# First 1024 tokens' keys, queries and half of the output gates by seven products of block sums, head norm folded into w_out, left operands split one by one, 43 working tiles

## The chip, the cores and the metric

The kernel runs on one core of a Trainium2 chip. The metric is the device time of one launch in microseconds (us). Three runs of the kernel before took 2398.47, 2396.38 and 2397.98 us; their median is 2397.98 us. The profile is of one more execution.

## The reference

One encoder layer on 2048 tokens of width 1024, in float32. The part that matters here is the mLSTM mixer at its start:

```python
xn = rmsnorm(h, norm_mix)
u = xn @ w_in                                  # 2048 x 1024 times 1024 x 3088
q, k, v, o, g = split(u, [512, 1024, 2048, 3072])
k = k * 128 ** -0.5                            # 4 heads of 128
h_fwd = mlstm_scan(q, k, v, g[0], g[1])        # 16 chunks of 128 tokens
h_bwd = flip(mlstm_scan(flip(q), flip(k), flip(v), flip(g[2]), flip(g[3])))
h = h_fwd + h_bwd
h = h * rsqrt(mean(h ** 2 per head) + EPS) * head_norm
h = h * sigmoid(o)
mix = h @ w_out
```

After it come a residual add, a square-ReLU MLP (1024 to 4096 to 1024), a gated embedding term and a last norm.

## The kernel before, in words

**Products.** Every float32 product is made of three TensorE products. An operand is split into a rounded high part (`hi`, cast by ScalarE, the profile's ACT) and a rest (`lo`, subtracted by VectorE, DVE), and `mm3` issues hi·hi, hi·lo and lo·hi into one PSUM bank. A 128x512 output over 1024 inputs thus takes 8 x 3 = 24 matmuls.

**Two ways to multiply.** A *slab job* (`slab_job`, `feat_group`) takes 128 columns of `w_in` and gives them for 1024 tokens in two groups of 24 matmuls, named `psf`. A *pair job* (`pair_job`, `products`) takes 256 columns for 1024 tokens as a 2 by 2 block product with seven block products in place of eight (`SEVEN`): sums S1 to S4 of the left blocks (the weights) and T1 to T4 of the right blocks (the tokens), each product 12 matmuls, named `pa`, `pb`, `pc`. One pair job is 84 matmuls; the two slab jobs with the same output are 96. `Left.preps` makes the sums (tiles `sa`) and splits them (tiles `op`) in six steps: S1 and S2 are split as one 128x1024 operand, and S3 and S4 as another. `run7` runs pair jobs one after another and weaves the next job's six steps between the current job's seven products.

**Order of the first stage.** The second 1024 tokens come first: values (`psv`), then keys, queries and all output gates in eight pair jobs (`pairs1`, with T1 to T4 made by `TokensA`). Then the first 1024 tokens: values; then slab jobs, four for the keys (k), six for the output gates (o0 to o5), the first halves of the four query slabs (`qa`); and last `fin`, a list written out by hand (`TR`) that holds the slabs o6 and o7 and the other query halves (`b0` to `b3`) beside the loads and splits of `w_out` (`a0`.., `c0`..) and the first forward chunk. The token tiles of the first half are prepared during `pairs1` by `Early`: norm, transposition in blocks through DRAM (`mix_d`), and `tr`, which multiplies by the norm gain and splits.

**The backward scan.** From the last group of values on, 15 backward state updates are laid between the slabs (`bwd_steps`: load `kt` and `vst`; split v into `vh`, `vl` and scale keys into `wk`; 12 matmuls `pu`, new state `Cn`, split into `Chi`, `Clo`, stored to `cb_d`). Each update is three steps, and the list `slots` says before which slab group a step stands. Stores of the first half's keys, queries and gates and of `cb_d` go through GpSimd's queue (POOL), loads through SyncE's queue (SP). Both are served in order.

**Later stages.** 14 forward chunks with the output projection (`pso`), then 32 pair jobs for the MLP's first matrix (`up_job`, whose sums are made on POOL at L468 to L474 and whose class `Left1` is a `LeftW`), then the second matrix (`down_job`, `Left2`), then the last stage.

**Gates and head norm.** `o_evac` and `o_pair` take the sigmoid on ACT and multiply by `head_norm` on DVE (`g_hn`). The rows of `w_out` are split without a factor.

**Buffers.** Working tiles of 4 KiB a partition come from one pool `H` of 39 (`NH`), load tiles from a pool `O` of 7. A scheduler puts the instructions of each engine in a fixed order when the program is built, by priority and by tiles that are free; on the chip every engine runs its list in that order and waits at each instruction for what it needs. All calls through the recording class have line L98 or L100 in the profile.

Of the kernel before, what the change touches and what calls it, by code (L numbers as in the profile page):

```python
# [16 lines left out]
P = 128  # L17
# [4 lines left out]
H = 4  # L22
# [7 lines left out]
NH = 39  # L30
# [5 lines left out]
def hybrid_mlstm_kernel(  # L36
# [216 lines left out]
    class Prep:  # L253
# [50 lines left out]
        def norm1(self, j):  # L304
# [4 lines left out]
            for g, sl in rowc["mix"]:  # L309
                V.scalar_tensor_tensor(xs[:, sl], self.raw[j][:, sl], r[:, 0:1], g, op0=ALU.mult, op1=ALU.mult)  # L310
# [53 lines left out]
    class Early(Prep):  # L364
# [3 lines left out]
        def __init__(self, load, gain, name):  # L368
            super().__init__(load, gain)
            self.d = dram.tile([32, 32, 4, P], F32, name=name)  # L370
            self.z = [None] * 4

        def norm(self):
# [5 lines left out]
            for j in range(4):  # L379
                V.tensor_scalar_mul(self.raw[j], self.raw[j], r[:, j:j + 1])  # L380
# [9 lines left out]
        def tr(self, k):  # L390
            t = Ht("xT", [P, 2, 512], F32R)
            g = self.gain[:, k:k + 1]
            z = self.z[k // 2][:, k % 2]
            A.activation(t[:, 0], z, AF.Copy, scale=g)
            V.scalar_tensor_tensor(t[:, 1], z, g, t[:, 0].bitcast(F32), op0=ALU.mult, op1=ALU.subtract)
# [53 lines left out]
    class Left:  # L449

# [4 lines left out]
        def preps(self, eng, eng2=None):  # L455
# [29 lines left out]
            by_row = lambda x, i, k: x[:, i, k]  # L485
            return [s12, op(["A11"], lambda: self.r[0][:, :, :P], by_col),
# [8 lines left out]

# [27 lines left out]

    class Job7:
# [4 lines left out]

    def run7(jobs, deep=None):  # L530

        def dma(i):
            if i < len(jobs):
                jobs[i].left.dma()
        for i, j in enumerate(jobs):
            if i == 0:
                dma(1)
            if deep is None or i + 2 <= deep:
                dma(i + 2)
            if deep is not None and i + 2 >= deep:  # L540
                dma(i + 3)
            nxt = jobs[i + 1].prep if i + 1 < len(jobs) else []

            def both(g, post):
                def f():
                    g()
                    for h in post:
                        h()
                return f
            weave([both(g, p_) for g, p_ in zip(j.groups, j.post)], nxt + j.side)  # L550
# [15 lines left out]
    kty = {}  # L566

    def store(c, dst, src):
        (SP if c >= 8 else G).dma_start(dst, src)

    def k_shuffle(t, h, c0):

        for m in range(2):
            if h == 0:
                kty[c0, m] = Ht("y", [P, 8, H, 32])
            y = kty[c0, m]
            V.transpose(y[:, :, h, :], t[:, 2 * m:2 * m + 2].rearrange("p c (b i) -> p (c b) i", i=32))
            if h == H - 1:
                for a in range(4):
                    (G if c0 >= 8 else SP).dma_start(kt_d[(c0 + 2 * m) * P:(c0 + 2 * m + 2) * P, a].rearrange("(b i) e -> i b e", i=32),  # L580
                                y[32 * a:32 * a + 32].rearrange("i b h j -> i b (h j)"))
                del kty[c0, m]

    def kq_evac(qk, h):
        def f(ps, c0):
            t = St("ev", [P, 4, P])
            tv = as_(ps, t)
            if qk == 0:
                A.activation(tv, ps, AF.Copy, scale=DK ** -0.5)
            else:  # L590
                V.tensor_copy(tv, ps)
            store(c0, kq_d[c0:c0 + 4, :, qk, h, :].rearrange("c p t -> p c t"), t)
            if qk == 0:
                k_shuffle(t, h, c0)
        return f

    def o_evac(j):
        def f(ps, c0):
            t = St("ev", [P, 4, P])
            act(as_(ps, t), ps, AF.Sigmoid)  # L600
            V.tensor_scalar_mul(t, t, gains["hn"][:, j:j + 1])
# [181 lines left out]
    def v_load(c):  # L783
        t = Ht("vst", [P, D])
# [27 lines left out]
    def bwd_steps(c):  # L812
        s = {}

        def load():
            s["kt"] = kt_load(c, Ot)
            s["v"] = v_load(c)
# [14 lines left out]
    ta_d = dram.tile([4, 2, P, 2, 512], F32, name="ta_d")  # L832

# [56 lines left out]
    def pair_job(B_, blk, col, finish, scale=None):  # L890

        e = {}

        def after(i, ps):
            t = St("ev", [P, 512])
            if i in (0, 2, 3, 6):
                if scale is None:
# [867 lines left out]
```

## Time and profile before

| | us |
|---|---|
| median of three runs | 2397.98 |
| the profiled execution, its own time | 2398.35 |
| its span on the core | 2396.6 |
| PE (TensorE matmul) busy | 2364.5 |
| DVE (VectorE) busy | 1565.9 |
| ACT (ScalarE) busy | 1165.9 |
| POOL (GpSimd) busy | 629.9 |

Times of the trace are counted from the span's start. 1.75 us of the execution's own time lie outside of the span. PEld is the weight load, which overlaps PE. A group's "mean ns of one" is the length of one instruction; matmuls overlap their neighbours, so that the distance from one start to the next is the cost of one, and not its length.

### The profile page before, as it was taken

The page shows a single profiled execution, that of the slowest core. Times are in us where ns is not written, and L with a number is a line of the kernel's source. Part 1 is how long each engine was busy: PE and PEld are TensorE (multiplying, and loading weights), DVE is VectorE, ACT ScalarE, POOL GpSimd, SP SyncE. Part 2 cuts the span into 40 slices and gives each one's busy share as a digit, 9 for nine tenths or more (in the row PEclk, how much of TensorE's full clock was granted, in tenths as well). Part 3 has the DMA queues.
Part 4 walks back from the last instruction along what each step waited for, and adds up shares of the span by engine and source line. Part 5 has one row for each costly group of instructions (what it writes and reads, how often), then busy time and mean ns, then how long its engine had stood idle before and what let it go on. Part 6 is the DMA issues. An engine that isn't in the chain of part 4 may idle for free.

```text
span 2396.6 us, 31587 instructions
## 1 busy us (share of the span) xinstructions
PE 2364.5 (99%) x11225; PEld 1951.6 (81%) x11225; DVE 1565.9 (65%) x2612; ACT 1165.9 (49%) x2168; POOL 629.9 (26%) x679
## 2 busy tenths in 40 slices
PE   8999999999999999999999999999999999999998
PEld 6988988788889887888888888787888888888886
DVE  6677545557778887567685544767666667666665
ACT  5234434437788874343353333444444444455554
POOL 0041121124333324446533332111111111111121
PEclk9999999999999999999999999999999999999999
DMA  5676656868768883456673332568686776796453
GB/s 168 229 230 191 192 149 222 281 222 291 232 226 294 276 269 110 132 174 206 213 228 106 106 113 73 174 135 195 143 188 165 170 170 154 173 217 176 136 138 87
DMA packets 273896, 440.66 MB, mean 184 GB/s; under 512 B 48921, under 2 KB 182425, under 8 KB 273738
## 3 DMA queue, kind: packets, MB, share of 16 engines
q1 hardware_dynamic: 211466, 308.48, 39.5%
q0 software_dynamic: 61984, 129.64, 23.3%
q8 instruction: 88, 1.44, 0.3%
q14 instruction: 70, 0.57, 0.1%
q10 hardware_dynamic: 288, 0.52, 0.1%
HBM read 262.87 MB, written 175.50 MB: 183 GB/s over the span
## 4 chain that ended last, share of the span: by engine, by line
PE 59%; DVE 1%; issue 1%; DMA 0%; ACT 0%; POOL 0%; ACTq 0%; DVEq 0%; POOLq 0%
PE pa L100 29%; PE pb L100 14%; PE pg L100 7%; PE pc L100 7%; PE pl L100 2%; DVE op L100 0%; DMA wst<-in_mlp_w 0%; DVE raw L100 0%; DVE z L100 0%; DVE e L100 0%; ACT op L100 0%; PE pt L100 0%; ACT e L100 0%; DVE h L100 0%; POOL sa L474 0%
## 5 line engine op out<-in xcount | busy, mean ns | idle before, releaser
L100 PE MATMUL pa<-op 128*128 128x512 f32 x3360 | 823.6, 394 | 3.9 <-ACT e L100 2.3
L100 PEld LDWEIGHTS pa<-op 128*128 128x128 f32 x3360 | 629.4, 188 | 155.9 <-ACT e L100 4.8
L100 PE MATMUL pb<-op 128*128 128x512 f32 x1632 | 407.5, 394 | 0.8 <-DVE op L100 0.8
L100 PEld LDWEIGHTS pb<-op 128*128 128x128 f32 x1632 | 306.1, 188 | 73.3 <-DVE op L100 1.1
L100 DVE TENSOR_TENSOR op<-sa,op 128x1024 fp32r<-128x1024 f32 (+2 forms) x176 | 188.9, 1079 | 142.3 <-ACT op L100 109.2
L100 ACT CAST op<-sa 128x1024 fp32r<-128x1024 f32 (+2 forms) x176 | 156.6, 895 | 188.0 <-PE pb L100 95.2
L1303 POOL DMA_DIRECT2D h_d<-o x96 | 94.9, 1033 | 529.5 <-DVE o L100 443.4
L100 ACT COPY e<-pa 128x512 f32<-128x512 f32 x160 | 93.8, 587 | 277.6 <-PE pa L100 277.0
L100 PE MATMUL pc<-op 128*128 128x512 f32 x768 | 191.8, 394 | 0.2 <-DVE op L100 0.2
L100 PEld LDWEIGHTS pc<-op 128*128 128x128 f32 x768 | 144.1, 188 | 34.4 <-DVE op L100 0.6
L100 PE MATMUL psf<-xT,whi 128*128 128x512 f32 x512 | 161.5, 396 | 0.0
L100 PE MATMUL psv<-whi,xT 128*128 128x272 f32 (+2 forms) x720 | 160.9, 317 | 0.0
L100 ACT CAST op<-wst 128x512 fp32r<-128x512 f32 x112 | 92.5, 834 | 114.4 <-DVE op L100 59.9
L100 DVE TENSOR_TENSOR op<-wst,op 128x512 fp32r<-128x512 f32 x112 | 123.7, 1107 | 31.4 <-ACT op L100 18.0
L468 POOL TENSOR_TENSOR sa<-wst 128x512 f32<-128x512 f32 x32 | 58.8, 1837 | 263.9 <-PE pb L100 167.3
L100 PEld LDWEIGHTS psv<-whi,xT 128*128 128x128 f32 x720 | 118.3, 188 | 9.2 <-ACT xT L100 0.3
L100 PE MATMUL psv<-wlo,xT 128*128 128x272 f32 (+2 forms) x360 | 113.8, 316 | 0.0
L100 PEld LDWEIGHTS psf<-xT,whi 128*128 128x128 f32 x512 | 95.8, 189 | 21.5
L100 DVE TENSOR_TENSOR op<-hst,op 128x384 fp32r<-128x384 f32 (+1 forms) x96 | 65.4, 687 | 64.6 <-ACT op L100 45.1
L100 PE MATMUL pso<-whi,hThi 128*128 128x512 f32 x256 | 102.2, 400 | 2.9 <-ACT nt L100 1.4
L100 PE MATMUL psf<-xT,wlo 128*128 128x512 f32 x256 | 101.4, 396 | 0.0
L100 PE MATMUL pg<-whi,xTh 128*128 128x512 f32 x256 | 101.3, 397 | 0.0
(267 smaller groups left out, 4378.6 us busy)
## 6 DMA issues: line engine op xcount, KB each, us to landing
wst<-in_mlp_w SPq DMA_DIRECT2D x96, 512.0 KB, 4.9
h_d<-o POOLq DMA_DIRECT2D x96, 512.0 KB, 14.0
hid_d<-e SPq DMA_DIRECT2D x128, 256.0 KB, 2.4
hst<-hid_d SPq DMA_DIRECT2D x64, 384.0 KB, 7.0
wst<-in_mlstm_w_in SPq DMA_DIRECT2D x44, 512.0 KB, 5.6
vst<-v_d SPq DMA_DIRECT2D x31, 512.0 KB, 4.6
raw<-in_x SPq DMA_DIRECT2D x16, 512.0 KB, 6.7
kq<-kq_d SPq DMA_DIRECT2D x16, 512.0 KB, 3.6
```

Source lines behind the costliest of these rows:

```text
L100: r = f(*a, **kw)
L468: eng.tensor_tensor(s[:, 0], r1[:, :, P:], r2[:, :, P:], op=add_)
L1303: G.dma_start(rows(h1_d, 2 * q + i), o[i], accum_op=add_)
```

## The change

1. The first 1024 tokens' keys, queries and output gates o0 to o3 become six pair jobs (`pairs0`). Their T1 to T4 are made on POOL from the tiles in `mix_d` while `pairs1` runs and are kept in DRAM (`tm_d`); the plain right blocks are the token tiles themselves (`Mixed`). Their left sums are made on POOL (`left.preps(G)`). `Early` now multiplies by the norm gain in its norm, so `tr` is a plain split.
2. `fin` holds the slabs o4 to o7, both halves, in place of o6, o7 and the query halves. Four token tiles (first half of the inputs of tokens 512 to 1023), which no pair job reads, are dropped and loaded again for them.
3. The backward updates are side steps of the six pair jobs, four steps in each and three in the second.
4. For every left operand made from weights (`pairs1`, `pairs0` and the 32 `up` jobs) S1 to S4 are split one by one (`single`): three steps stand in the job before, three in the job itself.
5. `head_norm` goes into the split of `w_out`; the gates' DVE multiply is gone.
6. `NH` is 43, and the GpSimd DMA scratch is 4096 bytes a partition. A chunk's load of `cb_d` is issued behind its mask (`dma_c`); the backward `vst` uses pool `O`.

```diff
-NH = 39
+NH = 43
...
     class Left:
-
+        single = False
...
+            if n > 2 and self.single:
+                sums = {"S1": lambda: self.s[0][:, 0], "S2": lambda: self.s[0][:, 1],
+                        "S3": lambda: self.s[1][:, 0], "S4": lambda: self.s[1][:, 1]}
+                sop = {nm: op([nm], f, one) for nm, f in sums.items()}
+                return [[s12, op(["A11"], lambda: self.r[0][:, :, :P], one)],
+                        [op(["A12", "A22"], lambda: self.r[1], by_col)],
+                        [s34, sop["S2"]], [sop["S1"]], [sop["S3"]], [sop["S4"]]]
...
+    class Mixed(Summed):
+        def get(self, nm, k):
+            if nm[0] == "B":
+                pr, k = self.e[int(nm[2]) - 1], k + 4 * (int(nm[1]) - 1)
+                return pr.hi[k], pr.lo[k]
+            return super().get(nm, k)
...
+    LEAD = 3
...
+            if j.left.single:
+                for at, fs in enumerate(j.prep[LEAD:]):
+                    main[at][:0] = fs
+            nxt = []
+            if nx and nx.left.single:
+                for at, fs in enumerate(nx.prep[:LEAD]):
+                    main[7 - LEAD + at][:0] = fs
+            elif nx:
+                nxt = nx.prep
...
     def o_evac(j):
...
             act(as_(ps, t), ps, AF.Sigmoid)
-            V.tensor_scalar_mul(t, t, gains["hn"][:, j:j + 1])
...
-        return Job7(left, B_, 4, after)
+        return Job7(left, B_, 4, after, None if blk else left.preps(G))
...
+    def wo_prep(k):
+        wo[k].prep(None, gains["hn"][:, k:k + 1])
...
-        jobs[b, "k"] = [slab_job(pa[b], b, KC + h * P, kq_evac(0, h)) for h in range(H)]
-        jobs[b, "q"] = [slab_job(pa[b], b, QC + h * P, kq_evac(1, h), (ps_mm, (ps_tr, ps_mm)[b])) for h in range(H)]
-        jobs[b, "o"] = [slab_job(pa[b], b, OC + j * P, o_evac(j)) for j in range(KD)]
+    jobs[0, "o"] = o = [slab_job(pa[0], 0, OC + j * P, o_evac(j)) for j in range(4, KD)]
...
+    def pairs_of(B_, b, n):
+        return [kq_pair(B_, b, qk, hp) for qk in range(2) for hp in range(2)] + [o_pair(B_, b, jp) for jp in range(n)]
+    pairs1, pairs0 = pairs_of(xa, 1, 4), pairs_of(xm, 0, 2)
...
+    for job, n in zip(pairs0, (4, 3, 4, 4, 4, 4)):
+        job.side += steps[at:at + n]
+        at += n
...
-    run(seq)
+    run([jobs[0, "v"][1], jobs[0, "v"][0]])
+    run7(pairs0)
+    run([fin])
...
-    nc = _bacc.Bacc("TRN2", target_bir_lowering=False, num_devices=1)
+    nc = _bacc.Bacc("TRN2", target_bir_lowering=False, num_devices=1, dynamic_dma_scratch_size=4096)
```

Over the whole program TensorE's list has 11,159 matmuls before and 11,087 after: 576 `psf` fewer, 504 `pa`, `pb` and `pc` more.

The first place is GpSimd's list where the keys of the first 1024 tokens begin. Before (`v_d`, `kq_d` and `cb_d` are stores of values, of keys and queries, and of backward states):

```order
L569 DMA v_d<-ev 4x32x512 x2
L828 DMA cb_d<-Chi 128x1032
L828 DMA cb_d<-Clo 128x1032
L569 DMA kq_d<-ev 128x4x128 x2
L828 DMA cb_d<-Chi 128x1032
```

and after:

```order
L864 DMA cb_d<-Chi 128x1032
L864 DMA cb_d<-Clo 128x1032
L466 TENSOR_TENSOR sa<-wst 128x512
L632 DMA kq_d<-ev 128x4x128
L467 TENSOR_TENSOR sa<-sa,wst 128x512
L632 DMA kq_d<-ev 128x4x128 x2
L471 TENSOR_TENSOR sa<-wst 128x512
L472 TENSOR_TENSOR sa<-wst,sa 128x512
```

A queue that held only stores now also holds the four block sums of the next pair job, between stores that wait for evacuated tiles.

The second place is DVE's list in the same stretch. Before (`ev` are evacuated tiles, `y` the transposed keys, `wlo` the rests of the next slab's weights):

```order
L100 COPY ev<-psv 128x512
L100 SCALAR_TENSOR_TENSOR Cn<-Cn,dcb,pu 128x258 x4
L100 TENSOR_TENSOR Clo<-Cn,Chi 128x1032
L100 TENSOR_TENSOR wlo<-wst,whi 128x1024
L100 STREAM_TRANSPOSE y<-ev 128x8x32 x2
L100 MEMSET vh 128x4x2
```

and after, in the first pair job:

```order
L100 TENSOR_TENSOR ev<-pc,ev 128x512
L100 STREAM_TRANSPOSE y<-ev 128x8x32 x2
L100 TENSOR_TENSOR op<-z,op 128x1024 x2
L100 TENSOR_TENSOR op<-sa,op 128x512
L100 TENSOR_TENSOR op<-z,op 128x1024 x2
L100 SCALAR_TENSOR_TENSOR Cn<-Cn,dcb,pu 128x258 x4
L100 TENSOR_TENSOR ev<-pa,ev 128x512
L100 TENSOR_TENSOR ev<-pb,ev 128x512
L100 TENSOR_TENSOR Clo<-Cn,Chi 128x1032
```

Between two backward updates DVE now has splits of T3 and T4 (`op<-z`), splits of left sums (`op<-sa`) and adds of products (`ev`), where it had one weight split and two transposes.

The third place is ACT's list in `fin`. Before (`mb` are the first chunks' decay masks, an exponential; `ev<-psf` here is a gate's sigmoid):

```order
L100 ACTIVATE ev<-psf 128x512
L100 ACT_TABLE_LOAD
L100 ACTIVATE mb<-mb,gcol 128x128 x9
L100 CAST pTh<-mb 128x512
L100 ACTIVATE mb<-mb,gcol 128x128 x2
```

and after:

```order
L100 ACTIVATE ev<-psf 128x512 x3
L100 ACT_TABLE_LOAD
L100 ACTIVATE mb<-mb,gcol 128x128 x8
L100 ACT_TABLE_LOAD
L100 ACTIVATE ev<-psf 128x512
L100 ACT_TABLE_LOAD
L100 ACTIVATE wk<-kt,wcol 128x128 x4
L100 CAST pTh<-mb 128x512 x2
```

Sigmoids and exponentials now alternate in `fin`, and ACT's list has 43 table loads in all where it had 37.

251 lines of the change are left out of this document (119 added, 132 removed).

## The prediction

> **What bounds the kernel now.** I read the page first, then busy time by stage, then waits and timeline where a stage is not full.
>
> ```profile
> span 2396.6 us, 31587 instructions
> PE 2364.5 (99%) x11225; PEld 1951.6 (81%) x11225; DVE 1565.9 (65%) x2612; ACT 1165.9 (49%) x2168; POOL 629.9 (26%) x679
> ```
>
> PE is busy for all but 32.1 us of its span. A gain must come from fewer matmuls, or from shorter ones; the other engines matter only where they become late. By stage (columns: busy us and count of PE, PEld, DVE, ACT, POOL; granted clock; share of the DMA engines; GB/s):
>
> ```profile
> 113.90:270.00 156.10, 156.10 (x676) 126.18 (x675) 105.28 (x175) 73.84 (x111) 37.73 (x64) 1.00 0.70 215
> 367.40:521.70 154.30, 151.76 (x710) 125.31 (x709) 88.73 (x193) 63.33 (x103) 32.19 (x50) 0.99 0.74 243
> 521.70:620.00 98.30, 93.42 (x500) 78.75 (x499) 66.04 (x117) 63.88 (x158) 40.34 (x48) 1.00 0.78 270
> 907.00:1440.00 533.00, 530.29 (x2284) 427.90 (x2283) 332.76 (x350) 205.57 (x288) 232.55 (x160) 1.00 0.49 155
> ```
>
> These are the pair jobs of the second half; the slab jobs that the change replaces, from the first `psf` to the last one ahead of o6 (I call it the middle stage); `fin` with the first chunks; and the first MLP matrix. The pair jobs leave PE no idle time with DVE at 67%. The middle stage has 2.54 us idle, `fin` and after it 4.88, the `up` jobs 2.71.
>
> What one matmul costs is seen in the timeline, from start to start. Two rows of slab work and two of pair work:
>
> ```profile
> 400.37 0.63 PE L100 MATMUL psf<-xT,whi 128*128 128x512 f32 x2
> ...
> 419.18 0.63 PE L100 MATMUL psf<-xT,whi 128*128 128x512 f32 x2
> ```
>
> ```profile
> 1001.88 5.70 PE L100 MATMUL pa<-op 128*128 128x512 f32 x24
> 1007.42 2.94 PE L100 MATMUL pc<-op 128*128 128x512 f32 x12
> ```
>
> Between the first two lie 27 rounds of three matmuls: 18.81 / 81 = 0.232 us each. The 24 of the pair job take 5.54 us, 0.231 each. Both ways pay the same for a matmul.
>
> **The matmuls removed.** Twelve slabs (4 k, 4 q, o0 to o3) of 48 matmuls are 576; six pair jobs of 84 are 504. 72 x 0.232 = 16.7 us leave PE, and PE is the path there, so this is the gain unless others are late. The built order has exactly 72 fewer, so a rival by which the saving isn't made has no chance.
>
> **What a wait costs.** The middle stage had one, for the operands of a backward update:
>
> ```profile
> PE pu L100 <- ACT wk L100: 2.0, 1, 2.0
> PE pu L100 <- DVE vl L100: 0.6, 1, 0.6
> ```
>
> ```profile
> 436.69 0.39 PE L100 MATMUL pu<-vh,wk 128*128 128x258 f32 x1 [1.97 <-ACT wk L100]
> 437.65 0.39 PE L100 MATMUL pu<-vl,wk 128*128 128x258 f32 x1 [0.57 <-DVE vl L100]
> ...
> 439.60 1.05 PE L100 MATMUL psf<-xT,whi 128*128 128x512 f32 x2
> ...
> 440.88 1.05 PE L100 MATMUL psf<-xT,whi 128*128 128x512 f32 x2
> ...
> 442.14 0.63 PE L100 MATMUL psf<-xT,whi 128*128 128x512 f32 x2
> ```
>
> PE waited 1.97 + 0.57 = 2.54 us. Behind that, two rounds took 1.28 and 1.26 us in place of 0.70, so another 1.1 us went to a halved clock. One late update is thus 3.7 us. The cause stands in two windows:
>
> ```profile
> 425.00:435.00 10.00, 9.72 (x42) 7.51 (x40) 1.72 (x2) 1.06 (x3) 2.47 (x4) 1.00 1.01 377
> 435.00:445.00 10.00, 7.74 (x31) 6.37 (x32) 8.04 (x20) 6.63 (x13) 1.86 (x3) 0.83 0.80 282
> ```
>
> The DMA engines were full for 10 us, DVE and ACT idle and waiting for data, and then all came at once. [...]
>
> This wait goes with the slabs: -3.7. What is late next are the updates in their new place.
>
> **DVE in the middle stage.** Of its 88.7 us these go:
>
> ```profile
> L100 DVE TENSOR_TENSOR wlo<-wst,whi 128x1024 fp32r<-128x1024 f32 x15 | 18.0, 1218 | 0.4 <-ACT whi L100 0.4
> L100 DVE TENSOR_SCALAR ev<-ev,g_hn 128x512 f32<-128x512 f32 x12 | 5.8, 484 | 12.4 <-ACT ev L100 12.3
> L100 DVE COPY ev<-psf 128x512 f32<-128x512 f32 x3 | 2.1, 689 | 7.2 <-PE psf L100 7.2
> ```
>
> Four of the weight splits (4.9) stay for o4 to o7, so 21.0 us go. What comes is priced by the pair jobs of the second half:
>
> ```profile
> L100 DVE TENSOR_TENSOR op<-wst,op 128x512 fp32r<-128x512 f32 x6 | 4.1, 689 | 3.3 <-ACT op L100 3.3
> L100 DVE TENSOR_TENSOR op<-wst,op 128x1024 fp32r<-128x1024 f32 x6 | 7.3, 1224 | 2.7 <-ACT op L100 2.4 <-PE pb L100 0.3
> L100 DVE TENSOR_TENSOR ev<-pa,ev 128x512 f32<-128x512 f32 x6 | 4.1, 692 | 3.9 <-PE pa L100 3.9
> L100 DVE TENSOR_TENSOR op<-z,op 128x1024 fp32r<-128x1024 f32 x4 | 4.8, 1210 | 0.8 <-ACT op L100 0.8
> ```
>
> A job splits A11 and S1 to S4 (5 x 0.689), A12 with A22 (1.224), and adds three products (3 x 0.692): 6.75 us, six jobs 40.5. T3 and T4 add 4.8, the four token tiles split again 2.8. DVE then has 88.7 - 21.0 + 48.1 = 115.8 us to do while PE has 154.3 - 2.5 - 1.1 - 16.7 = 134.0. That alone is 86%.
>
> The left sums on POOL are new beside it. The `up` jobs show what that does:
>
> ```profile
> L100 DVE TENSOR_TENSOR op<-wst,op 128x1024 fp32r<-128x1024 f32 x26 | 37.2, 1432 | 10.5 <-DMA wst<-in_mlp_w 5.2 <-PE pb L100 3.9 <-PE pa L100 0.9
> L100 DVE TENSOR_TENSOR op<-wst,op 128x512 fp32r<-128x512 f32 x26 | 27.7, 1067 | 9.6 <-ACT op L100 8.5
> L468 POOL TENSOR_TENSOR sa<-wst 128x512 f32<-128x512 f32 x26 | 46.9, 1802 | 183.8 <-PE pb L100 133.1 <-PE pa L100 29.9 <-DVE op L100 13.8
> L474 POOL TENSOR_TENSOR sa<-wst,sa 128x512 f32<-128x512 f32 x26 | 40.1, 1543 | 0.0
> ```
>
> The same two splits take 0.378 and 0.208 us more there. Five short ones and a long one are 2.1 us a job, 12.6 for six: 128.4 of 134.0 us, 96%. The two key jobs have T3 and T4 (4.8) and all the transposes:
>
> ```profile
> L100 DVE STREAM_TRANSPOSE y<-ev 128x256 f32<-128x256 f32 x16 | 6.2, 422 | 11.0 <-ACT ev L100 11.0
> ```
>
> Without these 11.0 us a job has 117.4 / 6 = 19.6 us of DVE for 134.0 / 6 = 22.3 of PE, 88%; a key job on average 25.1, 113%.
>
> DMA is no better off. The stage moved 243 GB/s x 154.3 us = 37.5 MB at share 0.74. The same stores, states and loads, plus 2 MB for T3 and T4, in 134 us are 295 GB/s, a share of 0.90 if it grows alike; the keys' transposed stores also become twice as many of half the size. The 10 full us above came at 377.
>
> So some updates will be late. Below: none, 0. Above: each of the 11 in the stage, 11 x 3.7 = 41. I take two, one in each key job, since DVE is over 100% in those alone: +7.4. PE's list is fixed, so behind a late update the whole next product waits; DVE's `Cn` and the store to `cb_d` wait with it.
>
> **`fin`.** The matmuls are the same in number. ACT gets six more table loads, and four more evacuations that DVE had:
>
> ```profile
> L100 ACT ACT_TABLE_LOAD x1 | 1.3, 1283 | 0.0
> ```
>
> 6 x 1.283 = 7.7 us. ACT was busy 65% of the 98.3 us, so most lie beside PE's work. Where PE already waited for the first chunk's chain, they don't:
>
> ```profile
> PE pn L100 <- DVE xt L100: 1.4, 1, 1.4
> PE pso L100 <- ACT nt L100: 1.4, 1, 1.4
> ```
>
> Below, DVE's waits vanish with its multiplies: -1.4. Above, all loads: +7.7. I take two loads, those ahead of the second chunk's exponentials: +2.6.
>
> **The rest, each at nothing.** Splitting S1 to S4 one by one costs DVE 4 x 0.689 - 2 x 1.224 = 0.3 us a job, covered in the `up` jobs by 200 us of idle DVE; from -2.7 (their idle time) to +3.7 (one late operand). The sums on POOL and the gain in `Early`'s norm fall in the second half's pair jobs, where DVE has 51 us to spare; 0 to +3.7. Head norm in the split of `w_out` changes a subtraction into a subtraction with a factor. The load of `cb_d` behind the mask has most of a chunk, some 20 us, to land. [...]
>
> **Sum.** -16.7 - 3.7 + 7.4 + 2.6 = -10.4. The profiled execution took 2398.35, the median is 0.37 lower: 2397.98 - 10.4 = 2387.6.
>
> **Rivals.**
>
> *No update is late and ACT's loads are hidden.* For it: in the chunks after 620 us DVE and ACT were both busy 80% and PE lost under 2 of 287 us (below). Against: 96% isn't 80%. 2397.98 - 20.4 = 2377.6. Chance 0.18.
>
> ```profile
> 620.00:907.00 287.00, 285.06 (x1721) 251.48 (x1720) 228.29 (x458) 229.41 (x613) 96.93 (x122) 1.00 0.77 256
> ```
>
> *The gain is spent.* About five late updates, 18.5, plus 2.6 against 20.4: 2398.7. For it: the DMA share of 0.90. Against: an update's loads are issued a whole update ahead, and 11 us of matmuls lie between most updates. Chance 0.20.
>
> *DVE becomes the bound of the middle stage, and the kernel is slower.* Let a sum on POOL keep DVE out for its whole time. The two rows of L468 and L474 give (1.802 + 1.543) / 2 = 1.67 us, 24 sums 40.1, so DVE needs 155.9 us for 134.0 of PE. The 21.9 us between are waits of 2.54 us, 8.6 of them, and each brings its 1.1 of slow clock, 9.5 more: 2397.98 - 20.4 + 21.9 + 9.5 + 2.6 = 2411.6. It decides from the fifth late update on, where 18.5 + 2.6 pass 20.4; from the seventh the loss passes 0.2%. Against: in the `up` jobs the splits lengthen by 2.1 us a job, not by the 6.7 us of four sums. Chance 0.10. [...]
>
> **How the numbers follow.** My forecast has 0.52. A measurement of this kernel can tell 0.2%, 4.8 us, from no change. All of the first rival and most of the forecast's own spread (no to three late updates, 2380 to 2392) lie below 2393.2; the second rival lies mostly within 4.8 us; the third above. Faster 0.71, same 0.19, slower 0.10. The range, 2378 to 2400, leaves out the third rival and the edges of the other two.
>
> **What would show it.** In the profile after: 504 matmuls of pair jobs between the last values and `fin` at 0.232 us from start to start; DVE busy 120 to 130 us in that stage; one to three waits of PE for `wk` or `vl` of 2 to 3 us, in the key jobs, each with a dip of the granted clock; `op<-sa` splits near 1.0 us there, not 0.69; 1 to 4 us more idle PE in `fin`. Wrong if PE is full in that stage, if waits stand in the later jobs too, if POOL's sums and not the updates are late, or if the `up` jobs, which get the same finer splits, gain or lose more than 3 us.

## The result, and the profile after

The kernel after takes 2507.65 us, median of four runs (2505.88 to 2509.3); the kernel before took 2397.79 beside it. The ratio is 1.0459, its 95% interval 1.0441 to 1.0477. The forecast was 2387.6, the range ended at 2400, so the kernel is 4.6% slower where a gain of 0.4% was expected. The page of the profile after:

```profile
span 2507.0 us, 31765 instructions
PE 2391.3 (95%) x11153; PEld 1964.1 (78%) x11153; DVE 1631.0 (65%) x2706; ACT 1212.4 (48%) x2312; POOL 671.2 (27%) x719
```

PE is idle for 2507.0 - 2391.3 = 115.7 us, where it was 32.1. And it is busy 26.8 us longer although 72 matmuls, 16.7 us, are gone: 43.5 us of matmuls at a lower clock (mean granted clock 0.977, before 0.997). 83.6 + 43.5 - 16.7 = 110.4 us, the difference of the spans. The matmuls were saved as forecast; the loss is waits, and for every two us of added waiting here about one more of slow clock.

Busy time by stage, in the columns of the prediction. The rows are the second half's pair jobs, the first half's values, the middle stage, the stage from o4 to the first output product, and the `up` jobs:

```profile
114.00:298.60 184.60, 161.81 (x675) 128.63 (x674) 113.47 (x180) 78.15 (x130) 60.33 (x80) 0.94 0.72 221
298.60:402.50 103.90, 98.47 (x619) 89.50 (x618) 51.02 (x110) 32.30 (x60) 28.91 (x39) 0.97 0.50 147
402.50:579.40 176.90, 153.01 (x650) 121.58 (x649) 129.68 (x228) 87.79 (x151) 59.71 (x67) 0.91 0.70 230
579.40:665.60 86.20, 67.53 (x334) 57.06 (x333) 38.58 (x57) 50.07 (x101) 27.69 (x36) 0.90 0.68 236
978.40:1640.30 661.90, 644.60 (x2746) 517.80 (x2745) 412.47 (x498) 250.24 (x410) 238.30 (x172) 0.99 0.45 142
```

Beside PE no engine is full in any of these stages: in the middle stage DVE is busy 129.7 of 176.9 us, and the DMA share is 0.70 where it was 0.74. The loss isn't one bound in one stage. It stands in six stages (these five and the chunks of the table below), four of which the prediction had put at nothing or had in no term. The four largest groups of PE's waits have different releasers (us in total, times, longest):

```profile
PE pa L100 <- ACT op L100: 13.9, 3, 11.5
PE pa L100 <- DVE op L100: 13.8, 6, 5.3
PE pu L100 <- DVE vh L100: 11.5, 4, 5.4
PE pS L100 <- DMA kq<-kq_d: 8.4, 1, 8.4
```

For the comparison of many kernels I measure stages from PE's first matmul of one kind to its first of the next: from the first `pa` to the first `psv` (pairs), to the last `psv` (values), to three slab groups ahead of the first `pS` (middle), to the first `pso` (o4 stage), to the first product of the `up` jobs (chunks), and to the first of the `down` jobs (up). What lies ahead (113 to 114 us), the `down` jobs (626 to 631) and the last stage (236 to 238) hardly move and are left out.

| kernel | pairs | values | middle | o4 stage | chunks | up | whole run |
|---|---|---|---|---|---|---|---|
| before | 156.1 | 96.1 | 155.8 | 64.4 | 304.3 | 640.8 | 2397.8 |
| after | 184.6 | 103.9 | 177.0 | 86.1 | 312.9 | 661.9 | 2507.7 |
| b_scratch | 156.0 | 96.1 | 155.8 | 64.4 | 304.2 | 640.7 | 2397.9 |
| b_fine | 158.5 | 96.0 | 155.4 | 64.4 | 304.1 | 649.6 | 2407.5 |
| b_nh42 | 156.0 | 96.1 | 155.7 | 65.7 | 309.9 | 650.4 | 2415.5 |
| b_hn | 156.0 | 96.2 | 155.8 | 64.8 | 303.6 | 641.2 | 2398.3 |
| b_upv | 156.0 | 96.1 | 155.8 | 64.4 | 304.2 | 638.8 | 2396.7 |
| a_no9 | 176.8 | 103.6 | 170.8 | 86.4 | 314.1 | 648.3 | 2483.2 |
| a_coarse_no9 | 163.5 | 106.0 | 184.5 | 86.2 | 312.8 | 649.4 | 2484.2 |
| a_no11 | 173.9 | 102.4 | 166.4 | 87.7 | 311.9 | 656.6 | 2478.2 |
| a_dma0 | 189.9 | 105.0 | 190.2 | 87.2 | 313.9 | 665.4 | 2533.0 |
| a_no11_dma0 | 173.6 | 103.2 | 169.7 | 87.3 | 315.3 | 655.8 | 2483.7 |
| a_fin | 184.5 | 104.0 | 172.9 | 80.7 | 308.7 | 662.0 | 2493.8 |
| c_swap | 175.2 | 103.7 | 160.4 | 84.0 | 315.1 | 655.6 | 2472.4 |
| c_sumsv0 | 163.1 | 106.8 | 165.4 | 81.2 | 311.9 | 655.2 | 2462.8 |
| c_onv | 175.4 | 102.3 | 150.4 | 81.5 | 315.9 | 656.7 | 2461.1 |
| d_mid | 161.4 | 108.0 | 144.1 | 84.6 | 314.0 | 655.5 | 2447.8 |
| d_all | 161.3 | 107.2 | 144.2 | 85.6 | 312.7 | 639.1 | 2429.2 |
| e_nosig | 161.8 | 106.0 | 143.9 | 71.2 | 308.4 | 639.0 | 2410.3 |

Names with b are the kernel before with one edit, those with a, c, d and e the kernel after with one or more. From before to after: pairs +28.5, values +7.8, middle +21.2 (37.9 over what 16.7 us fewer matmuls should have made of it), o4 stage +21.7, chunks +8.6, up +21.1. All edited kernels but the one measured in rounds (b_upv5, below) are single runs; the kernel before, run beside each of them, took 2397.5 to 2399.4. Stages of this table that an edit of the kernel before doesn't touch repeat within 0.5 us; the values stage of b_upv5 was 1.4 us longer.

### The profile page after: what moved, and what is told of

Read it like the earlier page. It is cut to its first block, busy times and chain, and to the rows that moved or that the text cites. A ratio compares the mean times of both kernels' runs of the same rounds, so it can differ in the third digit from the quotient of the medians.

```text
span 2507.0 us, 31765 instructions
## 1 busy us (share of the span) xinstructions
PE 2391.3 (95%) x11153; PEld 1964.1 (78%) x11153; DVE 1631.0 (65%) x2706; ACT 1212.4 (48%) x2312; POOL 671.2 (27%) x719
## 4 chain that ended last, share of the span: by engine, by line
PE 69%; issue 12%; DVE 7%; DMA 5%; POOL 3%; ACT 3%; SPq 0%; DVEq 0%; ACTq 0%; POOLq 0%
PE pa L100 24%; PE pb L100 12%; PE pg L100 7%; PE pc L100 6%; PE psv L100 6%; PE pso L100 5%; PE pn L100 2%; DVE op L100 2%; PE pl L100 2%; PE pu L100 2%; POOL h_d L1309 1%; DMA h_d<-o 1%; DMA wst<-in_mlp_w 1%; PE psf L100 1%; DMA ib<-in_d 1%
## 5 line engine op out<-in xcount | busy, mean ns | idle before, releaser
L100 PE MATMUL pa<-op 128*128 128x512 f32 x3576 | 890.9, 399 | 26.8 <-ACT e L100 7.4
L100 PEld LDWEIGHTS pa<-op 128*128 128x128 f32 x3576 | 676.8, 190 | 194.4 <-ACT e L100 9.5
L100 PE MATMUL pb<-op 128*128 128x512 f32 x1704 | 425.4, 395 | 0.9 <-DVE op L100 0.7
L100 PEld LDWEIGHTS pb<-op 128*128 128x128 f32 x1704 | 320.0, 188 | 77.6 <-DVE op L100 1.4
L100 DVE TENSOR_TENSOR op<-sa,op 128x512 fp32r<-128x512 f32 (+1 forms) x280 | 235.4, 851 | 94.9 <-ACT op L100 79.9
L100 ACT CAST op<-sa 128x512 fp32r<-128x512 f32 (+1 forms) x280 | 184.5, 668 | 228.7 <-PE pb L100 112.6
L100 DVE TENSOR_TENSOR op<-wst,op 128x512 fp32r<-128x512 f32 x124 | 137.0, 1106 | 103.9 <-PE pb L100 67.8
L100 PEld LDWEIGHTS pc<-op 128*128 128x128 f32 x768 | 144.2, 188 | 33.9
L100 PE MATMUL psv<-whi,xT 128*128 128x272 f32 (+2 forms) x720 | 161.4, 318 | 0.0
L100 PE MATMUL pso<-whi,hThi 128*128 128x512 f32 x256 | 102.3, 400 | 7.3 <-ACT nt L100 6.6
L100 ACT CAST op<-hst 128x384 fp32r<-128x384 f32 (+1 forms) x96 | 56.9, 621 | 97.9 <-PE pb L100 69.6
L100 PE MATMUL pso<-whi,hTlo 128*128 128x512 f32 x256 | 101.5, 397 | 0.4 <-DVE hTlo L100 0.4
L100 PE MATMUL pso<-wlo,hThi 128*128 128x512 f32 x256 | 101.6, 397 | 0.0
L100 PE MATMUL pg<-wlo,xTh 128*128 128x512 f32 x256 | 100.8, 394 | 0.0
```

Source lines behind the costliest of these rows:

```text
L100: r = f(*a, **kw)
```

## The experiments

### The parts of the change alone, in the kernel before

The expectations call theories by letters, and say what each letter means. Four edits that the prediction had at nothing, each alone but for the last, which needs the first beside it. The scratch:

```diff
-    nc = _bacc.Bacc("TRN2", target_bir_lowering=False, num_devices=1)
+    nc = _bacc.Bacc("TRN2", target_bir_lowering=False, num_devices=1, dynamic_dma_scratch_size=4096)
```

> The kernel before with only the GpSimd DMA scratch cut to 4096 bytes a partition. Theory R (the small scratch holds GpSimd's DMA issues, and what is queued behind them comes late): slower by 20 us or more, spread over all stages, the chunks and the second matrix too. Theories W (left weights are loaded too late), F (the finer splits leave operands just in time) and M (VectorE is the bound of the middle stage, with GpSimd's sums beside it): 2398, within 3 us.

2397.94 us, no stage moved. Theory R falls.

The finer splits (part 4 with its `run7` and later weight loads):

```diff
+        single = True
...
+                return [[s12, op(["A11"], lambda: self.r[0][:, :, :P], one)],
+                        [op(["A12", "A22"], lambda: self.r[1], by_col)],
+                        [s34, sop["S2"]], [sop["S1"]], [sop["S3"]], [sop["S4"]]]
```

> The kernel before with only part 4 of the change: S1 to S4 split one by one, three steps in the job itself, and with it the later load of the weights that its run7 makes. F and W: the 32 up jobs take about 20 us more (641 to 661, as in the kernel after) and the second half's pair jobs 3 to 10 more, so 2420 to 2430 in all. W alone adds: the long wait of 11.5 us in the second half's pair jobs does not come, since the loads for GpSimd's token sums, behind which the weights were queued, are not there. M and R: within 3 us of 2398.

2407.48. They cost 8.9 us in the `up` jobs and 2.4 in the pair jobs: real, but under half of the 21 us that the `up` jobs lose in the kernel after. F and W are too weak alone.

Head norm in the split of `w_out`:

```diff
-            V.tensor_scalar_mul(t, t, gains["hn"][:, j:j + 1])
...
+    def wo_prep(k):
+        wo[k].prep(None, gains["hn"][:, k:k + 1])
```

> The kernel before with only part 5 of the change, the head norm in the split of w_out and no multiply of the gates. As the prediction had it: nothing, 2396 to 2400, with the stage from the last slabs on at 64 us and the chunks at 304. If it is part of the loss: stage and chunks together longer by 3 us or more.

2398.25; the two stages together are 0.3 us shorter. Nothing, as forecast.

More tiles, with the small scratch that makes room for them:

```diff
-NH = 39
+NH = 42
...
-    nc = _bacc.Bacc("TRN2", target_bir_lowering=False, num_devices=1)
+    nc = _bacc.Bacc("TRN2", target_bir_lowering=False, num_devices=1, dynamic_dma_scratch_size=4096)
```

> The kernel before with 42 tiles in H in place of 39 and the small scratch that makes room for them; no work is changed. Theory E (with more free tiles GpSimd starts its left sums earlier, just then when VectorE has the splits that TensorE waits for): the up jobs take 645 to 652 in place of 641, 2402 to 2410 in all. Else 2398, within 3 us.

2415.45: three more tiles, no work changed, and the kernel before is 17.5 us slower than its neighbour run (9.6 in the `up` jobs, as theory E had it, and 5.6 in the chunks, which it had not). The small scratch alone had moved nothing. The same place of the first `up` job shows how. The kernel before (here and below: start, us, engine; the bracket is idle time and who ended it):

```profile
916.24 1.21 DVE L100 TENSOR_TENSOR z<-z 128x1024 f32<-128x1024 f32 x1
917.38 2.35 DVE L100 TENSOR_TENSOR op<-z,op 128x1024 fp32r<-128x1024 f32 x2
917.60 10.10 POOL L473 TENSOR_TENSOR sa<-wst 128x512 f32<-128x512 f32 x1 [8.17 <-DVE z L100]
918.64 2.83 PE L100 MATMUL pa<-op 128*128 128x512 f32 x11 [0.63 <-DVE op L100]
```

and b_nh42:

```profile
922.02 1.62 POOL L473 TENSOR_TENSOR sa<-wst 128x512 f32<-128x512 f32 x1 [6.43 <-DVE z L100]
922.40 2.32 DVE L100 TENSOR_TENSOR z<-z 128x1024 f32<-128x1024 f32 x1
923.60 2.25 POOL L474 TENSOR_TENSOR sa<-wst,sa 128x512 f32<-128x512 f32 x1
924.64 3.42 DVE L100 TENSOR_TENSOR op<-z,op 128x1024 fp32r<-128x1024 f32 x2
926.99 3.36 PE L100 MATMUL pa<-op 128*128 128x512 f32 x7 [2.87 <-DVE op L100]
```

DVE's instructions are the same in the same order. POOL's sum starts 0.38 us ahead of the second `z<-z`, where it stood 1.36 us behind that one's start, and then `z<-z` takes 2.32 us in place of 1.21 and the two splits 3.42 in place of 2.35. PE, which takes these splits just in time, waits 2.87 us in place of 0.63. In the kernel before it was POOL that was kept out, 10.10 us for one sum, while DVE ran back to back. Here lies the first cause: where a sum on POOL and DVE instructions with two inputs in SBUF met in these rows, one side was held back (DVE by 1.1 us twice in b_nh42; POOL by some 8 in the kernel before, whose next sum took 1.29), and a change that only moved POOL by less than 2 us moved PE. This is one place; that all of the 17.5 us come about so isn't shown.

### Tiles and queues: the second half's pair jobs

In the kernel after, the largest wait of all stands in the pair jobs of the second half, where the T sums of the first half are now made. The queue of SP there:

```profile
230.15 5.75 SPq L632 DMA_DIRECT2D og_d<-ev  x3
236.08 1.45 SPq L353 DMA_DIRECT2D z<-mix_d  x3
237.62 1.10 SPq L511 DMA_DIRECT2D wst<-in_mlstm_w_in  x2
```

The loads of the next job's weights (L511) leave SP only at 237.6, behind gate stores that wait for evacuations and behind the loads for the sums. ACT, DVE and PE wait for them (the same timeline, by engine):

```profile
245.04 0.62 ACT L100 CAST op<-wst 128x512 fp32r<-128x512 f32 x1 [9.52 <-DMA wst<-in_mlstm_w_in]
...
246.54 2.77 DVE L100 TENSOR_TENSOR sa<-wst 128x512 f32<-128x512 f32 x1 [14.36 <-DMA wst<-in_mlstm_w_in]
249.23 2.98 DVE L100 TENSOR_TENSOR op<-wst,op 128x512 fp32r<-128x512 f32 x1
252.13 0.68 DVE L100 TENSOR_TENSOR sa<-sa,wst 128x512 f32<-128x512 f32 x1
...
245.71 1.22 PE L100 MATMUL pa<-xT,op 128*128 128x512 f32 x2 [11.47 <-ACT op L100]
252.27 2.07 PE L100 MATMUL pa<-xT,op 128*128 128x512 f32 x4 [5.34 <-DVE op L100]
```

Once the data is there, POOL's T sums (2.35 us each) run at the same time, and the DVE instructions of 0.68 us take 2.77 and 2.98. Several edits tried to tell the tiles, the place of the load and the sums themselves apart:

```diff
-NH = 43
-NO = 7
+NH = 41
+NO = 9
```

> The kernel after with 9 tiles in pool O and 41 in H, in place of 7 and 43. W: loads on SyncE's queue wait less for a free tile, the second half's pair jobs lose most of their 22.8 us of idle TensorE (under 8 left), the time falls to 2475 to 2490. F, R and M: 2507, within 5 us.

2483.20: 24.5 us back, in the range that theory W gave, but by luck, since they don't come where it said: the pair jobs still idle 15.9 us. 13.6 us come from the `up` jobs, the rest from pairs and middle.

> The kernel after with part 4 undone (S1 with S2 and S3 with S4 split together, all six steps in the job before, weights loaded at the start of a job two ahead), and 9 tiles in O, 41 in H, since more loads are under way. F and W: the up jobs return to 641 (within 4 us), the second half's pair jobs to under 165; 2450 to 2470 in all. M: the middle stage stays near 177 us, for 134 of matmuls, since VectorE's work there is the same. R: nothing returns, 2500 or more.

Its edit beside the 41 and 9 tiles (and the two places ahead of a first job, which then make all six steps there):

```diff
-        single = True
+        single = False
```

2484.22, the same time as a_no9. The `up` jobs (649.4) don't return to 641; the pair jobs gain 13 us (weights are asked for earlier and splits done a job ahead; which of the two does it wasn't tested), and the middle stage loses 14. F falls as the main cause of the `up` jobs, and M's 177 was 184.5.

The same edit as a_no9 with 39 and 11:

> The kernel after with 11 tiles in O and 39 in H. Theory O (too few tiles in O hold SyncE's queue, which is served in order): the time falls on below the 2483 us of 9 and 41, by 5 to 20 us, most of it in the second half's pair jobs (176.8 us there) and the middle stage (170.8). Theory T (it is not the count of tiles but the place of the weight loads, one third of a job ahead): the second half's pair jobs stay within 4 us of 176.8. Either way the stage between middle stage and first output product (86 us) stays.

2478.23: the middle stage falls on to 166.4, the pairs only to 173.9. Theory O's total just came, 5 us below a_no9, but the pair jobs stay within the 4 us of theory T. A tile more in O is here also a tile less in H, and no run parts the two; by b_nh42, where H alone grew, the tiles of H can matter as much.

> The kernel after, pools of 7 and 43, with the left weights loaded at the start of a job for the job two ahead, as before the change, in place of the job's end. T: the idle 22.8 us of the second half's pair jobs fall under 6, the up jobs fall from 662 to 645 or less, 2460 to 2475 in all. O: four weight tiles are then under way in place of two, fewer are left for the token sums and the backward loads, and the middle stage gets longer by 5 us or more; in all within 15 us of 2507.

```diff
-                        main[6].append(jobs[t].left.dma)
+                        main[0][:0] = [jobs[t].left.dma]
```

2533.00, slower than the kernel after, with the middle stage at 190.2. That weights loaded earlier keep O's tiles from the backward loads, as O said, fits the middle stage, but wasn't traced, and the whole is 11 us over O's bound. The pair jobs gain nothing. T falls.

Both edits:

> The kernel after with both: 11 tiles in O and 39 in H, and the left weights loaded at a job's start for the job two ahead. O and T together: the second half's pair jobs at 156 to 160 us as before the change, the up jobs at 641 to 648, 2445 to 2460 in all; what is then left over before is in the middle stage and the stage behind it. Theory F (the finer splits themselves): the second half's pair jobs stay over 165.

2483.66, pairs 173.6: both together don't mend the pair jobs either. My 156 to 160 was wrong: the load's place and 11 tiles in O together don't bring this stage back.

The "two first edits" of the next expectations are 11 tiles in O with 39 in H (a_no11) and the first chunk's gate load behind the second chunk's loads (a_fin, below).

> The same two first edits, and the four token sums of the first half made on GpSimd during its values (v0) and no longer during the second half's pair jobs. Theory S (these sums, their loads on SyncE and GpSimd's four 2.3 us additions, are what the second half's pair jobs lose, with weights and splits late behind them): those fall from 174 to 157 to 160 us, the values lengthen by less than 5; 2448 to 2455. Theory F (the finer splits cost it): 170 or more, 2460 to 2466.

```diff
-    pairs1[4].side += xm.sums(0)
-    pairs1[5].side += xm.sums(1)
+    u0.side += xm.sums(0) + xm.sums(1)
```

2462.82. With the T sums in the values stage the pair jobs take 163.1 in place of 173.9, and the values 4.4 more. Theory S is right in kind, but the stage stays 3 us above its range. Edit by edit, 11 us of the 28.5 go with the sums' place, some 11 with the tiles (184.6 to 173.9), and 2.4 with the finer splits by b_fine; some 5 us stay unexplained. These shares aren't fixed: with the sums left in place, undoing the finer splits (a_coarse_no9) brought the stage to 163.5 as well. (The kernel with the first two edits alone wasn't run; the 2464 in the expectations is an estimate from two single edits, too low as the stages show, so I compare stages only.)

### The middle stage

> The same two first edits, and the left sums of the middle stage's six jobs made on VectorE in place of GpSimd. Theory X (a sum on GpSimd keeps VectorE out for its whole time): 24 sums of 0.68 us add 16 to VectorE, but the splits and updates beside them shorten by as much or more, the middle stage falls from 166 to 155 to 162. Theory D: VectorE is full, and the stage gets longer, 168 to 180.

```diff
-        return Job7(left, B_, 4, after, None if blk else left.preps(G))
+        return Job7(left, B_, 4, after)
```

2461.06; the stage takes 150.4 us in place of 165 to 166, below even the range of theory X. DVE was given 20 sums more in this window and is busy less. The stage in a_no11 (sums on POOL) and some of its DVE rows:

```profile
390.50:556.90 166.40, 147.79 (x650) 118.89 (x649) 130.63 (x227) 87.16 (x150) 57.59 (x67) 0.93 0.70 231
L100 DVE TENSOR_TENSOR op<-sa,op 128x512 fp32r<-128x512 f32 x23 | 19.3, 846 | 1.5 <-ACT op L100 1.5
L100 DVE SCALAR_TENSOR_TENSOR wk<-kt,wcol,wk 128x128 fp32r<-128x128 f32 x44 | 18.0, 469 | 3.3 <-ACT wk L100 3.0 <-issue 0.3
L100 DVE TENSOR_TENSOR op<-wst,op 128x1024 fp32r<-128x1024 f32 x5 | 13.6, 2722 | 0.0
```

and in c_onv (sums on DVE; `sa` are three rows of 6.8, 3.4 and 3.4 us, the first shown):

```profile
390.90:541.20 150.30, 139.48 (x649) 112.44 (x648) 122.35 (x246) 85.69 (x148) 30.49 (x47) 0.99 0.76 250
L100 DVE TENSOR_TENSOR op<-sa,op 128x512 fp32r<-128x512 f32 x23 | 15.4, 682 | 0.2 <-ACT op L100 0.2
L100 DVE SCALAR_TENSOR_TENSOR wk<-kt,wcol,wk 128x128 fp32r<-128x128 f32 x44 | 13.0, 348 | 4.4 <-ACT wk L100 4.4
L100 DVE TENSOR_TENSOR op<-wst,op 128x1024 fp32r<-128x1024 f32 x5 | 6.1, 1212 | 0.6 <-ACT op L100 0.6
L100 DVE TENSOR_TENSOR sa<-wst 128x512 f32<-128x512 f32 x10 | 6.8, 683 | 0.0
```

Without its 13.6 us of sums DVE is busy 108.8 us here and 130.6 there. One more `op<-z` falls into the window there, 1.2 us; the other 20.7 are lengthening, for 20 sums that kept POOL busy 27.7 (four rows of 6.4 to 7.9 us): three quarters of their time. In c_onv POOL's list holds only stores there, which then come earlier too, but that isn't what PE gained: in a_no11 no wait of PE, ACT or DVE in this stage is put down to a DMA. Which DVE instructions lengthen is seen by form. With two inputs in SBUF, `op<-sa` took 846 ns in a_no11 and 682 in c_onv, `wk` 469 and 348. With one input in PSUM, `ev<-pc,ev` took 690 and 687, and `Cn` 477 in both. Single rows of the kernel after agree: `ev<-pa,ev` took its 0.69 us at 549.99 beside a sum of 549.29 to 550.60, and `op<-wst,op` (128x1024) at 553.10 took 4.46 beside three sums of 552.67 to 556.47, where it takes 1.21 in c_onv. DVE was held back here, and in the kernel before it was POOL, with 10.10 us for one sum; what decides between them wasn't tested.

> The kernel after with 11 tiles in O and 39 in H, the second chunk's loads ahead of the first chunk's gate load, and in the middle stage the operands of a backward update (vh, vl, wk) made one step earlier, ahead of the update before it. By the two runs that had the first edits alone, 2478 - 14 = 2464 without the last one. Theory J (the updates' operands stand just ahead of the update in ScalarE's and VectorE's lists, behind an evacuation that waits for TensorE): the middle stage falls from 166 to 150 or less, the waits of pu under 5 us; 2445 to 2452. Theory D (VectorE has no time left there): the waits move to the products' splits, the stage stays within 5 us of 166.

```diff
+    for i in range(8, len(steps) - 1, 2):
+        steps[i], steps[i + 1] = steps[i + 1], steps[i]
...
-    for job, n in zip(pairs0, (4, 3, 4, 4, 4, 4)):
+    for job, n in zip(pairs0, (4, 2, 5, 4, 4, 4)):
```

2472.43, middle stage 160.4: 5 to 6 us, between both theories. What J meant is seen in a_no11:

```profile
470.51 0.59 ACT L100 COPY ev<-pa 128x512 f32<-128x512 f32 x1 [7.76 <-PE pa L100]
470.99 1.28 ACT L100 ACTIVATE wk<-kt,wcol 128x128 fp32r<-128x128 f32 x4
471.43 3.51 DVE L100 SCALAR_TENSOR_TENSOR wk<-kt,wcol,wk 128x128 fp32r<-128x128 f32 x4 [3.00 <-ACT wk L100]
472.68 1.05 ACT L100 CAST vh<-vst 128x1024 fp32r<-128x1024 f32 x1
473.77 1.23 PE L100 MATMUL pu<-vh,wk 128*128 128x258 f32 x4 [3.30 <-ACT vh L100]
```

ACT stood idle for 7.76 us in front of an evacuation, with the next update's `wk` and `vh` behind it in its list, and PE then waited 3.30 us for them. Neither DVE nor ACT is full; the operand is queued behind something that waits for PE.

All edits of c_swap, c_sumsv0 and c_onv together:

> The kernel after with 11 tiles in O and 39 in H, the second chunk's loads ahead of the first chunk's gate load, token sums of the first half in the values stage, left sums of the middle stage on VectorE, and the operands of each backward update made one step earlier. If the gains of the single edits add up (16 and 6 us in the middle stage, 11 in the second half's pair jobs, of 2464): middle stage 142 to 146 us, 2430 to 2442. If VectorE, now with 16 us more work, is full (theory D): middle stage 150 or more, no better than with the left sums moved alone.

2447.78; the stage at 144.1, as the sum of both edits had it. The whole is 6 us over my bound, since values and o4 stage didn't shrink. The middle stage now is 11.7 us shorter than before the change, of the 16.7 that are to be had.

### The up jobs

> The kernel of d_mid, and the left sums of the 32 up jobs made on VectorE too. Theory X (a GpSimd sum keeps VectorE out, and the up jobs lose by where it falls): the up jobs take 638 to 645 us in place of 655, 10 to 17 us less than d_mid. Theory F (finer splits come late whoever makes the sums): 650 or more.

```diff
-        return Job7(left, B_, 4, after, left.preps(G))
+        return Job7(left, B_, 4, after)
```

2429.16: the `up` jobs take 639.1 in place of 655.5, less than in the kernel before, with the finer splits. PE's idle time there falls from 14.5 us to 2.6. In d_mid and in d_all the squaring that ends a product, two SBUF inputs, in that order:

```profile
L100 DVE SCALAR_TENSOR_TENSOR e<-e 128x512 f32<-128x512 f32 x95 | 89.5, 942 | 1.1
L100 DVE TENSOR_TENSOR op<-wst,op 128x512 fp32r<-128x512 f32 x33 | 27.8, 844 | 13.2 <-ACT op L100 13.2
```

```profile
L100 DVE SCALAR_TENSOR_TENSOR e<-e 128x512 f32<-128x512 f32 x95 | 73.8, 777 | 1.1
L100 DVE TENSOR_TENSOR op<-wst,op 128x512 fp32r<-128x512 f32 x33 | 22.7, 687 | 3.8 <-ACT op L100 3.8
```

So the `up` jobs' loss, too, goes with POOL's sums. That the finer splits (b_fine, 649.6) and the tiles (b_nh42, 650.4) only shifted where the collision falls fits this; for the tiles it isn't shown, since d_all has 39 in H.

The same edit alone in the kernel before:

> The kernel before with only the left sums of the 32 up jobs made on VectorE in place of GpSimd. Theory X: the splits of 1.36 us shorten to 1.21, and the 4.0 us of idle TensorE and the slow clock behind them go: up jobs 634 to 640 in place of 641, 2391 to 2397. Theory D: VectorE's list gets 87 us longer and puts sums ahead of the adds that free PSUM: up jobs 643 to 655, slower than 2398.

2396.68, `up` jobs 638.8, 1.9 us shorter in a single run. In rounds:

> The kernel before with only the left sums of the 32 up jobs made on VectorE, again, in five rounds. Theory X, with 638.8 us for the up jobs in place of 640.7: faster by 1 to 3 us, ratio 0.9988 to 0.9996, the interval below 1. If the one look was chance: the interval holds 1.

2396.21, median of 11 runs, against 2397.53; ratio 0.9994, interval 0.9984 to 1.0003. The `up` jobs are again shorter (638.3), but the interval holds 1: a gain isn't shown.

### The stage from o4 on

> The kernel after with one edge more: the first chunk's gate load (og from og_d) is issued on SyncE behind the second chunk's loads. Theory Q (that load waited 23 us on SyncE's queue for the last gate store, and held the keys and queries of the second chunk behind it, for which TensorE waited 8.4 us): the stage from o4 to the first output product falls from 86 to 70 to 78 us and nothing else moves; 2493 to 2501 in all. Theory L (the stage is long by ScalarE's table loads and the late end of the middle stage): 84 to 87, 2507.

```diff
-            SP.dma_start(self.kq, kq_d[c])
+            self.ld = SP.dma_start(self.kq, kq_d[c])
...
             self.og = Ot("og", [P, KD, P])
-            SP.dma_start(self.og, og_d[c])
+            if c == 0:
+                with tc.issue_after(ch[1].ld.ins):
+                    SP.dma_start(self.og, og_d[c])
+            else:
+                SP.dma_start(self.og, og_d[c])
```

2493.78. The cause is in SP's waits of the kernel after:

```profile
SPq L1028 <- DMA og_d<-ev: 29.4, 2, 23.1
```

and in its queue and what held it:

```profile
603.59 0.78 POOL L632 DMA_DIRECT2D og_d<-ev  x1 [5.56 <-ACT ev L100]
606.50 0.33 SPq L1028 DMA_DIRECT2D og<-og_d  x1
...
609.51 0.39 SPq L1004 DMA_DIRECT2D kq<-kq_d  x1
```

The first chunk's gate load stood on SP for 23.1 us until the last slab's gates were stored, and the second chunk's `kq`, long stored, stood behind it. With the edit the 8.4 us wait for `kq` is gone (PE's idle time in the stage falls from 18.7 to 12.2 us) and the stage is at 80.7. Q is right on the wait and wrong on the size, 70 to 78: another wait, for `pTh`, takes 3.7 us of it. Nor did the rest stand still, as Q had it: the middle stage and the chunks are each some 4 us shorter, for a reason that wasn't traced.

That wait leads to ACT. In d_all the stage has 7 table loads where the kernel before had 1:

```profile
564.17 1.28 ACT L100 ACT_TABLE_LOAD   x1 [1.20 <-issue]
565.46 0.60 ACT L100 ACTIVATE ev<-psf 128x512 f32<-128x512 f32 x1
566.08 1.28 ACT L100 ACT_TABLE_LOAD   x1
567.37 1.28 ACT L100 ACTIVATE wk<-kt,wcol 128x128 fp32r<-128x128 f32 x4
568.56 1.12 ACT L100 CAST pTh<-mb 128x512 fp32r<-128x512 f32 x2
```

One gate of 0.60 us brings two loads, and the first chunk's `wk` and `pTh`, for which PE waits 3.67 us, stand behind them.

> The kernel of d_all with the sigmoid of the gates o4 to o7 of the first 1024 tokens left out (a plain copy in its place), so that ScalarE has no table loads between the first chunks' exponentials. If the table loads (7 of 1.28 us, 9.0 us in the stage) and the fixed order of sigmoids and exponentials make it long: the stage falls from 86 to 70 to 76 us, 2413 to 2420 in all. If it is long by the first chunks' own chain and the late end of the middle stage: 82 or more, 2425 to 2429.

```diff
-            act(as_(ps, t), ps, AF.Sigmoid)
+            A.copy(as_(ps, t), ps)
```

2410.30, for a kernel that leaves out a part of the layer: the stage falls from 85.6 to 71.2, and the chunks by 4.4. The windows of the stage, first d_all:

```profile
526.80:612.40 85.60, 70.75 (x345) 59.37 (x345) 45.92 (x65) 54.86 (x107) 32.15 (x39) 0.92 0.79 282
```

then e_nosig:

```profile
525.70:596.90 71.20, 66.96 (x345) 56.46 (x346) 42.18 (x65) 47.12 (x102) 31.95 (x39) 0.98 0.87 321
```

The 7.7 us less ACT work (six table loads of 1.28) shorten the stage by 14.4, since they stood in the chain ahead of PE: 10.6 us of waits, and 3.8 of slow clock behind them. The expected total (2413 and up) was still too high, by the chunks.

## Why the prediction was wrong

**What bounds the kernel; the matmuls removed.** Right. The saving is made, and PE is the path. But the idle time of DVE beside it was read as slack ("51 us to spare", "200 us of idle DVE"), when a PE that is 99% busy only says that its operands came in time, by a margin nowhere shown.

**What a wait costs.** Right in kind: 83.6 us of added idle time brought 43.5 us of slow clock, half a us for each, as 1.1 for 2.54 had it.

**DVE in the middle stage.** Its busy time was forecast at 128.4 us and measured at 129.7. That agreement is luck: by c_onv and a_no11 the work was 110.0 us and the lengthening 20.7, where the forecast had 115.8 and 12.6. The step that failed is what was made of it: "DVE is over 100% in those alone", so two late updates, 7.4 us. PE waited nine times for an update's operands (15.3 us), only twice of these in the key jobs, and seven times at a product, for an operand or an evacuation (8.6 us). The stage was 37.9 us over its 139 and DVE only 73% busy. A share of busy time says nothing of which instruction is late. The lengthening, put at 2.1 us a job from the means of the `up` jobs, was 20.7 us for the sums of five jobs, 4.1 each: three quarters of the time of POOL's sums, where the third rival had all of it, as an assumption. That rival came nearest on the mechanism (moving the sums gave 15 to 16 us), but was wrong on the condition: it needed no full DVE, only a DVE that is late for one split. Its 2411.6 is still 96 us short.

**"An update's loads are issued a whole update ahead."** It spoke against the second rival. With `vst` in pool O too, its loads did wait for tiles on SP: 30.0 us in six waits behind `wk`, the longest 16.1. But no wait of ACT or DVE in that stage is put down to a load of `kt` or `vst`; the updates' operands were late in the lists of ACT and DVE. The DMA share of 0.90, which spoke for that rival, was 0.70. Two or four tiles moved from H to O gave the middle stage 6 to 10.6 us; whether by the loads or by the smaller H stays open.

**`fin`.** Taken +2.6, top +7.7; measured +21.7. The six loads were counted right (7 for 1). Their place wasn't: two of them stand ahead of the operands that PE takes next, and the gates are evacuated in a fixed order with the exponentials (14.4 us with the slow clock). And the queue of SP, 5 to 6.5 us, was in no term.

**"The rest, each at nothing".** Here the largest part was lost. The finer splits in the `up` jobs were given -2.7 to +3.7 and cost 8.9 alone, 21.1 with the other edits; the cover "by 200 us of idle DVE" was the error: with the sums off POOL the same splits cost nothing (639.1), so it was not their work but where they met POOL's sums. The sums on POOL in the second half's pair jobs were given at most 3.7; that stage lost 28.5. The tiles were taken at 0: three of them cost the kernel before 17.5 us. The values (+7.8) and the chunks (+8.6) were in no term. Head norm and scratch were right at 0.

**The range.** The terms put at nothing were bounded by one late operand each, and `fin` by its table loads alone. The sums on POOL cost time in three stages at once (pairs, middle, `up`), and the order of the lists of SP and ACT in the o4 stage, so the errors had one sign and added up.

**Open.** Of d_all's 31 us over the kernel before, e_nosig explains 19. The values stage stays 11 us longer there, with a wait of 4.55 us for the first updates; the pair jobs some 5; the o4 stage 7 even without its sigmoids; the chunks some 4, with a wait of 0.51 us ahead of the output product in seven of them. None of these was traced by an experiment. Nor was what moving tiles from H to O does, 24 to 29 us of the loss in the kernel after. No version with the six pair jobs came out faster than the kernel before.

## What to carry to other kernels

A kernel at 99% of one engine is tuned in the order of all others: price an edit by what it puts ahead of the next operand on each in-order queue, not by busy time (here a gate load stood on SP for 23.1 us with `kq` behind it), and look for edits that move GpSimd beside VectorE instructions with two SBUF inputs (here `op<-sa` took 846 ns for 682). Move sums from GpSimd to VectorE where PE waits for VectorE: 0.68 us of work there can be cheaper than 1.4 us on GpSimd beside it. Count a wait of PE one and a half times (here 83.6 us of idle time brought 43.5 of slow clock), and treat more buffers as a change that can cost time (here three tiles cost 17.5 us).

## What was not expected of the hardware

- VectorE was busy less after it was given more: 122.4 us with 13.6 us of sums of its own, 130.6 with them on GpSimd.
- One 128x512 sum on GpSimd took 10.10 us beside a VectorE that ran back to back; two of its neighbours in b_nh42 took 1.62 and 2.25.
- Three more working tiles made the kernel before 17.5 us slower; the smaller scratch that goes with them moved nothing alone.
